# Turning the accumulated modulation of the next layer on VectorE instead of TensorE

## The chip, the core and the metric

The kernel runs on one core of a Trainium2 chip. A core has five engines that each work through their own list of instructions, strictly in order: TensorE (PE, with its weight loads shown as PEld), VectorE (DVE), ScalarE (ACT), GpSimd (POOL) and SyncE (SP), which here only issues transfers. An instruction that waits for a semaphore holds everything behind it on its engine. The metric is the device time of one execution in microseconds (us); of several runs the median counts.

## The reference, cut to what matters

The program is a two-layer trunk on 512 latent and 256 context tokens of width 1024. Each layer first derives a modulation (shift, scale and gate for two sub-layers, 6 x 1024 columns) from two vectors `c` and `c_ctx`, then does token mixing, then an MLP with 4096 hidden columns:

```python
mx = (silu_c @ w_ada[i] + b_ada[i])[:, None, :]      # latent tokens, 6*1024 columns
mc = silu_cc @ w_ada[i] + b_ada[i]                   # context tokens
...
x = x + gx1 * y_x                                    # token mixing
x = x + gx2 * sqrelu_mlp(modulate(rmsnorm(x, norm2_g[i]), sx2, ax2), w_mlp1[i], w_mlp2[i])
```

What the change touches is the product of two vectors with `w_ada[1]`, the modulation of the second layer. It is two rows of 6144 numbers, and the kernel needs them as columns: a number for each of 128 partitions, for 48 tiles of 128 columns and both kinds of token.

## The kernel before, in words

All matrices are float32 and are split into a high and a low part; a product is three matmuls (lines 107 to 109). Weights come in slabs of 256 columns (`r_w`), ScalarE makes the high part (`h_w`, line 76) and in layer 0 GpSimd the low part (`l_w`, line 77).

The MLP of layer 0 has four rounds. A round computes eight hidden tiles `f` from four slabs of `w_mlp1`, then adds eight tiles `r` from four slabs of `w_mlp2` to the residual stream `X`. I call one such slab a weight slab: TensorE does four blocks for it, two of 512 latent tokens (24 matmuls each) and two of 256 context tokens. An `f` block is emptied from PSUM by ScalarE into `fr` (three buffers, line 1211) and squared; VectorE then forms its low part `fl` (line 1214), which the `r` blocks need. An `r` block is emptied by VectorE alone, with the sum into `X` (line 1135); the latent blocks have two PSUM banks and the context blocks two more. In the names `f_0_4_0` and `r_0_2_512` the numbers are the round, the tile, and the first token of the block.

Between these blocks `ada_rows` works on the modulation of layer 1, in 24 modulation slabs of 256 columns, each loaded in two halves `ar` of 512 KB (line 245). `ar` has one buffer, so a load starts when the products of the half before it have read it. For each half and each of the two vectors, ScalarE (line 258, the first product of a slab) and VectorE (line 261) multiply by a number per partition and add up in `adaac`, a tile of 128 partitions by 512 numbers with four buffers in turn (tag `t2k`). After the two halves a slab's 1024 rows are folded into 128 partitions. What is left is a sum over partitions and a turn: TensorE transposes the four 128 x 128 pieces into a PSUM tile `adaps` (line 270), and VectorE reduces it (line 273) and adds the bias (line 275).

`ada_rows` is a generator; the MLP calls a step after a latent block, one half each. But this is only the order in which the program is written. Each engine's list is put together at build time by a scheduler that estimates times, so where a step stands on an engine's list follows from that estimate and from what it waits for, such as a free buffer.

Of the kernel before, what the change touches and what calls it, by code (L numbers as in the profile page):

```python
# [8 lines left out]
F32 = mybir.dt.float32  # L9
F32R = mybir.dt.float32r  # L10
AF = mybir.ActivationFunctionType
ALU = mybir.AluOpType
AX = mybir.AxisListType

P = 128
# [24 lines left out]
R_BADA, R_N1, R_N2, R_BG, R_BDW, R_LNG, R_LNB, R_ANG, R_C, R_CC, R_END = (  # L40
    0, 48, 56, 64, 80, 84, 88, 92, 93, 101, 109)
# [5 lines left out]
def f32(ap):  # L47
    return ap.bitcast(F32)
# [3 lines left out]
def trunk_kernel(  # L52
# [6 lines left out]
    nc = tc.nc  # L59
# [3 lines left out]
    cpool = ctx.enter_context(tc.tile_pool(name="cpool", bufs=1))  # L63
# [3 lines left out]
    spool = ctx.enter_context(tc.tile_pool(name="spool", bufs=2))  # L67
# [34 lines left out]
    def rows(src, col0, ncols):  # L102
        return src[:, col0 : col0 + ncols].rearrange("(k p) n -> p k n", p=P)
# [24 lines left out]
    nc.sync.dma_start(cst, consts[:, :C_COS])  # L128
    ident = cst[:, C_ID : C_ID + P]
    ones = cst[:, C_ONE : C_ONE + P]  # L130
    mhalf = cpool.tile([P, 8], F32, name="mhalf")
    nc.gpsimd.memset(mhalf, -0.5)

# [5 lines left out]
    state = {"behind": ()}  # L139
# [100 lines left out]
    def ada_rows(i, L):  # L240


        def load(n):
            r = state["rp"].tile([P, KT // 2, 256], F32, tag="araw", bufs=1, name=f"ar{i}_{n}")
            nc.sync.dma_start(r, rows(w_ada[i], 256 * (n // 2), 256)[:, 4 * (n % 2) : 4 * (n % 2) + 4])
            return r

        r = load(0)
        for n in range(48):
            s = n // 2  # L250
            if n % 2 == 0:
                a = state["tp"].tile([P, 512], F32, tag="t2k", bufs=state["nt"], name=f"adaac{i}_{s}")
                a = a.rearrange("p (q n) -> p q n", q=2)
            for j in range(4):
                k = 4 * (n % 2) + j
                for q in range(2):
                    if k == 0:
                        nc.scalar.activation(out=a[:, q], in_=r[:, j], func=AF.Copy,
                                             scale=cvec[:, k, q : q + 1])
                    else:  # L260
                        nc.vector.scalar_tensor_tensor(  # L261
                            out=a[:, q], in0=r[:, j], scalar=cvec[:, k, q : q + 1], in1=a[:, q],
                            op0=ALU.mult, op1=ALU.add)
            if n < 47:
                r = load(n + 1)
            yield
            if n % 2:
                ps = state["mi"](f"adaps{i}_{s}")
                for m in range(4):
                    nc.tensor.transpose(ps[:, m * P : m * P + P],  # L270
                                        a[:, m // 2, m % 2 * P : m % 2 * P + P], ident)
                ad = L["ad"][:, :, 2 * s : 2 * s + 2]
                nc.vector.tensor_reduce(out=ad, in_=ps.rearrange("p (q m k) -> p q m k", q=2, m=2),
                                        axis=AX.X, op=ALU.add)
                nc.vector.tensor_tensor(
                    out=ad, in0=ad,
                    in1=L["cols"][:, R_BADA + 2 * s : R_BADA + 2 * s + 2].unsqueeze(1)
                    .to_broadcast([P, 2, 2]), op=ALU.add)

    def ada_gain(L, which, ks=slice(0, KT)):  # L280
        par, r0, nm = ((1, R_N1, "A1"), (4, R_N2, "A2"))[which]
# [71 lines left out]
    for t in range(NTT):  # L353
# [4 lines left out]
        if t == 1:  # L358
            L = layer_params(0)
# [17 lines left out]
    for t in range(NTT):  # L377
        xn = xns[t]
        nc.scalar.activation(out=xn, in_=xrs[t], func=AF.Square, accum_out=rs[:, t : t + 1])
        r = rs[:, t : t + 1]  # L380
# [9 lines left out]
    for s in range(2):  # L390
        nc.vector.tensor_tensor(
            out=cvec[:, :, s], in0=L["cols"][:, R_C + 8 * s : R_C + 8 * s + 8],
            in1=sg[:, 8 * s : 8 * s + 8], op=ALU.mult)
# [36 lines left out]
    for i in range(DEPTH):  # L430
# [5 lines left out]
        cols = L["cols"]  # L436
# [480 lines left out]
        def ps_for(g, name):  # L917
            if g.start:
                return mc.tile([P, 512], F32, tag="mc", name=name)
            return mm_tile(name)  # L920
# [52 lines left out]
        for half, lst in ((1, ga), (0, gc)):  # L973
            for s in range(4):
# [6 lines left out]
                for m in range(2):  # L981
# [3 lines left out]
                    for g in groups:  # L985
                        W = g.stop - g.start
                        ps = ps_for(g, f"gt{i}_{half}_{mb}_{g.start}")
# [70 lines left out]
        for s in range(4):  # L1058
# [3 lines left out]
            for g in groups:  # L1062
                W = g.stop - g.start
                for m in range(2):
                    mb = 2 * s + m
                    ps = ps_for(g, f"ya{i}_{mb}_{g.start}")
                    fm_block(ps[:, :W], w, m * P, lambda k: (ah[:, k], al[:, k]), g)
                    nc.vector.tensor_tensor(out=ga[mb][:, g], in0=ga[mb][:, g], in1=ps[:, :W],
                                            op=ALU.mult)
# [12 lines left out]
        for cc in range(CT):  # L1082
            for a0, W, t0 in cgr:
                low = nc.vector.tensor_tensor(out=CL[:, cc, t0 : t0 + W],
                                              in0=ca[cc][:, a0 : a0 + W],
                                              in1=f32(CH[:, cc, t0 : t0 + W]), op=ALU.subtract)
        normed.append(low.ins)
        mh, ml = [None] * KT, [None] * KT
        for s in range(2):
# [7 lines left out]
            for m in range(4):  # L1097
                mb = 4 * s + m
                for g in groups:
                    W = g.stop - g.start  # L1100
                    ps = ps_for(g, f"yc{i}_{mb}_{g.start}")
# [3 lines left out]
                                            op=ALU.mult)  # L1105
                rr = {}
                for g in groups:
                    rr[g.start] = gp.tile([P, 512], F32, tag="ar", bufs=3,
                                          name=f"mr{i}_{mb}_{g.start}")[:, : g.stop - g.start]
                    nc.vector.tensor_tensor(out=rr[g.start], in0=ga[mb][:, g], in1=gc[mb][:, g],  # L1110
                                            op=ALU.add)
# [79 lines left out]
        if not last:  # L1191
            Ln = layer_params(i + 1)
            acc = xp.tile([P, NT], F32, tag="acc", name=f"acc{i}_3")
            rpool = tc.tile_pool(name="araw", bufs=1, reuse_waits="tile")
            state["rp"] = rpool.__enter__()
            ada_todo = ada_rows(i + 1, Ln)
            hh = hpool.tile([P, KT, NT], F32R, tag="hh", name=f"h1h_{i + 1}")
            hl = hpool.tile([P, KT, NT], F32R, tag="hl", name=f"h1l_{i + 1}")
# [80 lines left out]
        if not last:  # L1279
# [3 lines left out]
            L = Ln  # L1283
# [77 lines left out]
```

## Time and profile before

| what | value |
|---|---|
| median of 3 runs | 2370.24 us (2361.84 to 2371.28) |
| profiled execution, its own time | 2368.32 us |
| profiled execution, span from first to last instruction | 2366.5 us |
| TensorE / VectorE / ScalarE / GpSimd busy | 2286.9 / 1477.9 / 992.1 / 689.4 us |
| granted TensorE clock | 0.989 |
| line 270, transposes of `adaac` | 96 matmuls, 852 to 1317 us |
| line 261, VectorE products into `adaac` | 336, 183.0 us busy |

The MLP of layer 0 with the modulation work lies between about 760 and 1370 us of the span. Idle time of an engine costs something only where another one waits for it; so the views that name who ended a wait, and the chain of waits, matter more here than the busy shares.

### The profile page before, as it was taken

How to read it: one execution, taken by the hardware profiler on the slowest of the kernel's cores; microseconds unless marked ns; L12 is line 12 of the kernel's file. 1: busy time of each engine (PE TensorE's matmuls, PEld its weight loads, DVE VectorE, ACT ScalarE, POOL GpSimd, SP SyncE). 2: the span in 40 equal slices, each digit the busy share in tenths (PEclk: the TensorE clock that was granted, in tenths of full speed). 3: DMA queues.
4: the chain of work that ended last, by engine and by line, in shares of the span. 5: the costliest groups of instructions: out<-in, count | busy, mean ns of one | idle time of the engine just before them, and what ended most of it. 6: DMA issues, size and time to landing. Idle time of an engine off the chain costs nothing.

```text
span 2366.5 us, 36536 instructions
## 1 busy us (share of the span) xinstructions
PE 2286.9 (97%) x14698; PEld 2049.6 (87%) x14698; DVE 1477.9 (62%) x2581; ACT 992.1 (42%) x1965; POOL 689.4 (29%) x792
## 2 busy tenths in 40 slices
PE   7999999999999999999999998999999999999999
PEld 6999998888888988888888997999877879888887
DVE  6777776699666665555563366676759976433333
ACT  5555654522332353242514345555542333532432
POOL 2866754100000133232232365766610000000000
PEclk9999999999999999999999999999999999999999
DMA  9211111144535223334332211111123324232322
GB/s 306 60 43 35 44 45 44 46 159 135 173 114 186 84 81 124 117 115 133 108 112 85 90 55 56 43 43 41 43 76 126 129 88 127 82 97 92 104 89 71
DMA packets 222570, 224.76 MB, mean 95 GB/s; under 512 B 6256, under 2 KB 212544, under 8 KB 222272
## 3 DMA queue, kind: packets, MB, share of 16 engines
q1 hardware_dynamic: 222400, 222.43, 29.2%
q8 instruction: 115, 1.88, 0.3%
q14 instruction: 55, 0.45, 0.1%
HBM read 208.73 MB, written 13.67 MB: 94 GB/s over the span
## 4 chain that ended last, share of the span: by engine, by line
PE 81%; DVE 10%; DMA 3%; ACT 3%; POOL 2%; issue 1%; SPq 0%; ACTq 0%; DVEq 0%; POOLq 0%
PE r L107 6%; PE r L108 6%; PE r L109 6%; PE f L108 6%; PE f L107 6%; PE f L109 5%; PE gt L107 3%; PE gt L109 3%; PE gt L108 3%; PE qk L107 2%; PE qk L108 2%; PE qk L109 2%; PE v L107 2%; DVE adaac L261 2%; PE v L108 2%; PE v L109 2%
## 5 line engine op out<-in xcount | busy, mean ns | idle before, releaser
L108 PE MATMUL f<-h2l,h_w 128*128 128x512 f32 (+1 forms) x832 | 284.0, 343 | 3.8 <-DVE h2l L326 2.0
L107 PE MATMUL r<-fh,h_w 128*128 128x512 f32 (+1 forms) x832 | 283.9, 342 | 0.4 <-DVE X L1135 0.4
L107 PE MATMUL f<-h2h,h_w 128*128 128x512 f32 (+1 forms) x832 | 282.3, 343 | 2.0 <-ACT h2h L76 1.3
L108 PE MATMUL r<-fl,h_w 128*128 128x512 f32 (+1 forms) x832 | 283.2, 340 | 0.1
L109 PE MATMUL r<-fh,l_w 128*128 128x512 f32 (+1 forms) x832 | 282.9, 340 | 0.0
L109 PE MATMUL f<-h2h,l_w 128*128 128x512 f32 (+1 forms) x832 | 282.5, 341 | 0.0
L77 POOL TENSOR_TENSOR l_w<-r_w,h_w 128x1024 fp32r<-128x1024 f32 x64 | 158.1, 2492 | 348.4 <-ACT h_w L76 348.4
L261 DVE SCALAR_TENSOR_TENSOR adaac<-ar,cvec,adaac 128x256 f32<-128x256 f32 x336 | 183.0, 597 | 89.3 <-DMA ar<-in_w_ada_dram 64.2
L76 ACT ACTIVATE h_w<-r_w 128x1024 fp32r<-128x1024 f32 x128 | 128.5, 1051 | 261.5 <-PE r L108 117.2
L940 DVE SCALAR_TENSOR_TENSOR cacc<-z,cols,cacc 128x783 f32<-128x783 f32 (+1 forms) x240 | 201.1, 890 | 0.3
L107 PE MATMUL qk<-h_wqk,h1h 128*128 128x256 f32 x640 | 183.9, 289 | 5.1 <-ACT h1h L76 3.6
L108 PE MATMUL qk<-l_wqk,h1h 128*128 128x256 f32 x640 | 181.3, 285 | 0.0
L108 PEld LDWEIGHTS f<-h2l,h_w 128*128 128x128 f32 x832 | 158.3, 190 | 22.9 <-POOL h2l L77 3.0
L109 PE MATMUL qk<-h_wqk,h1l 128*128 128x256 f32 x640 | 177.1, 285 | 0.0
L107 PEld LDWEIGHTS f<-h2h,h_w 128*128 128x128 f32 x832 | 156.7, 190 | 20.6 <-ACT h2h L76 1.9
L109 PEld LDWEIGHTS f<-h2h,l_w 128*128 128x128 f32 x832 | 158.1, 190 | 17.7
L108 PEld LDWEIGHTS r<-fl,h_w 128*128 128x128 f32 x832 | 157.8, 190 | 17.5 <-DVE fl L1214 0.5
L109 PEld LDWEIGHTS r<-fh,l_w 128*128 128x128 f32 x832 | 157.6, 190 | 17.7
L107 PEld LDWEIGHTS r<-fh,h_w 128*128 128x128 f32 x832 | 157.6, 190 | 17.7 <-issue 0.5
L707 DVE TENSOR_REDUCE st<-S 128x1 f32<-128x768 f32 (+1 forms) x160 | 134.7, 846 | 61.1 <-PE S L705 60.0
L1135 DVE SCALAR_TENSOR_TENSOR X<-r,ad,X 128x512 f32<-128x512 f32 (+1 forms) x104 | 64.8, 625 | 172.8 <-PE r L109 172.5
L710 ACT ACTIVATE e<-S,st 128x768 f32<-128x768 f32 (+1 forms) x160 | 130.8, 820 | 36.3 <-DVE st L707 36.2
(253 smaller groups left out, 6245.2 us busy)
## 6 DMA issues: line engine op xcount, KB each, us to landing
r_w<-in_w_mlp_dram SPq DMA_DIRECT2D x64, 1024.0 KB, 5.5
ada<-in_w_ada_dram SPq DMA_DIRECT2D x24, 1024.0 KB, 5.8
ar<-in_w_ada_dram SPq DMA_DIRECT2D x48, 512.0 KB, 3.7
r_wqk<-in_w_in_dram SPq DMA_DIRECT2D x32, 512.0 KB, 5.2
r_wg<-in_w_in_dram SPq DMA_DIRECT2D x16, 1024.0 KB, 5.2
r_wv<-in_w_in_dram SPq DMA_DIRECT2D x8, 1024.0 KB, 5.2
r_wao<-in_w_attn_out_dram SPq DMA_DIRECT2D x8, 1024.0 KB, 5.2
r_wo<-in_w_out_dram SPq DMA_DIRECT2D x8, 1024.0 KB, 7.6
```

Source lines behind the costliest of these rows:

```text
L76: nc.scalar.activation(out=hi, in_=src, func=AF.Copy)
L77: (lo_eng or nc.vector).tensor_tensor(out=lo, in0=src, in1=f32(hi), op=ALU.subtract)
L107: nc.tensor.matmul(ps, sh, mh, start=first, stop=False)
L108: nc.tensor.matmul(ps, sh, ml, start=False, stop=False)
L109: nc.tensor.matmul(ps, sl, mh, start=False, stop=last)
L261: nc.vector.scalar_tensor_tensor(out=a[:, q], in0=r[:, j], scalar=cvec[:, k, q : q + 1], in1=a[:, q], op0=ALU.mult, op1=ALU.add)
L707: nc.vector.tensor_reduce(out=st[:, m : m + 1], in_=S[:, :nkey], axis=AX.X, op=ALU.max, negate=True)
L710: nc.scalar.activation(out=e[:, :nkey], in_=S[:, :nkey], func=AF.Exp, bias=st[:, m : m + 1], accum_out=st[:, 2 + m : 3 + m])
L940: nc.vector.scalar_tensor_tensor(out=ca[cc][:, :CV], in0=zt[cc][:, t : t + CV], scalar=wcol, in1=ca[cc][:, :CV], op0=ALU.mult, op1=ALU.add)
L1135: nc.vector.scalar_tensor_tensor(out=X[:, mb, g], in0=ps[:, :W], scalar=gate[:, s, mb : mb + 1], in1=X[:, mb, g], op0=ALU.mult, op1=ALU.add)
```

## The change

The transposes on TensorE go. When a slab's sum is complete, VectorE turns it in blocks of 32 by 32 into `adat` (the same `t2k` buffers) and reduces over the 32 numbers of each block into `part` (`adp` in the trace; one buffer, a tag shared with the norms' `dg`). That leaves four groups of 32 partitions to be added, which is done for eight slabs at once: four small products with `fold32`, a matrix of 128 x 32 that is made once at the start, write one PSUM tile, and one VectorE operation adds the bias for all eight slabs. So there are three folds, after modulation slabs 7, 15 and 23.

```diff
+    fold32 = cpool.tile([P, 32], F32, name="fold32")
+    nc.vector.tensor_reduce(out=fold32, in_=ident.rearrange("p (b r) -> p r b", b=4), axis=AX.X,
+                            op=ALU.add)
...
+        def fold(s0):
+            ps = state["mi"](f"adaps{i}_{s0}")
+            for c_ in range(4):
+                nc.tensor.matmul(ps[32 * c_ : 32 * c_ + 32, :32], fold32, part[:, c_],
+                                 start=True, stop=True, tile_position=(0, 32 * c_))
+            nc.vector.tensor_tensor(
+                out=L["ad"][:, :, 2 * s0 : 2 * s0 + 16].rearrange("p q (n m) -> p n q m", n=8),
+                in0=ps[:, :32].rearrange("p (n q m) -> p n q m", n=8, q=2),
+                in1=L["cols"][:, R_BADA + 2 * s0 : R_BADA + 2 * s0 + 16]
+                .rearrange("p (n m) -> p n m", n=8).unsqueeze(2).to_broadcast([P, 8, 2, 2]),
+                op=ALU.add)
...
             if n % 2:
-                ps = state["mi"](f"adaps{i}_{s}")
-                for m in range(4):
-                    nc.tensor.transpose(ps[:, m * P : m * P + P],
-                                        a[:, m // 2, m % 2 * P : m % 2 * P + P], ident)
-                ad = L["ad"][:, :, 2 * s : 2 * s + 2]
-                nc.vector.tensor_reduce(out=ad, in_=ps.rearrange("p (q m k) -> p q m k", q=2, m=2),
-                                        axis=AX.X, op=ALU.add)
-                nc.vector.tensor_tensor(
-                    out=ad, in0=ad,
-                    in1=L["cols"][:, R_BADA + 2 * s : R_BADA + 2 * s + 2].unsqueeze(1)
-                    .to_broadcast([P, 2, 2]), op=ALU.add)
+                if s % 8 == 0:
+                    part = spool.tile([P, 4, P], F32, tag="dg", bufs=1, name=f"adp{i}_{s}")[:, :, :32]
+                b = state["tp"].tile([P, 512], F32, tag="t2k", bufs=state["nt"], name=f"adat{i}_{s}")
+                nc.vector.transpose(out=b, in_=a.rearrange("p q n -> p (q n)"))
+                nc.vector.tensor_reduce(
+                    out=part[:, :, 4 * (s % 8) : 4 * (s % 8) + 4].rearrange("p c n -> p n c"),
+                    in_=b.rearrange("p (n c r) -> p n c r", n=4, c=4), axis=AX.X, op=ALU.add)
+                if s % 8 == 7:
+                    fold(s - 7)
```

Since the scheduler lays the lists anew, the change also moves instructions. On VectorE, in the first round's `r` blocks, this stood in the list before (`adaac_6` and `adaac_7` are modulation slabs 6 and 7, `ar_13` and `ar_14` halves of their weights):

```order
L261 SCALAR_TENSOR_TENSOR adaac_6_10713<-ar_13_10722,cvec,adaac_6_10713 128x256 x8
L1135 SCALAR_TENSOR_TENSOR X_8446<-r_0_2_0_10200,ad_139,X_8446 128x512
L1135 SCALAR_TENSOR_TENSOR X_8446<-r_0_3_0_10236,ad_139,X_8446 128x512
L1135 SCALAR_TENSOR_TENSOR X_8446<-r_0_2_512_10280,ad_139,X_8446 128x256
L1135 SCALAR_TENSOR_TENSOR X_8446<-r_0_3_512_10306,ad_139,X_8446 128x256
L1135 SCALAR_TENSOR_TENSOR X_8446<-r_0_4_0_10340,ad_139,X_8446 128x512
L1135 SCALAR_TENSOR_TENSOR X_8446<-r_0_5_0_10376,ad_139,X_8446 128x512
L273 TENSOR_REDUCE ad_9370<-adaps_3_10402 128x2x2
L261 SCALAR_TENSOR_TENSOR adaac_7_10869<-ar_14_10830,cvec,adaac_7_10869 128x256 x2
```

And this stands there with the change (line 277 is what was line 261, line 1149 what was 1135):

```order
L1149 SCALAR_TENSOR_TENSOR X_8448<-r_0_2_0_10195,ad_141,X_8448 128x512
L288 TENSOR_REDUCE adp_0_9946<-adat_6_10841 128x4x4
L277 SCALAR_TENSOR_TENSOR adaac_7_10844<-ar_14_10809,cvec,adaac_7_10844 128x256 x6
L1149 SCALAR_TENSOR_TENSOR X_8448<-r_0_3_0_10231,ad_141,X_8448 128x512
L1149 SCALAR_TENSOR_TENSOR X_8448<-r_0_2_512_10271,ad_141,X_8448 128x256
L277 SCALAR_TENSOR_TENSOR adaac_7_10844<-ar_15_10853,cvec,adaac_7_10844 128x256 x7
L1149 SCALAR_TENSOR_TENSOR X_8448<-r_0_3_512_10297,ad_141,X_8448 128x256
L277 SCALAR_TENSOR_TENSOR adaac_7_10844<-ar_15_10853,cvec,adaac_7_10844 128x256
L287 STREAM_TRANSPOSE adat_7_10993<-adaac_7_10844 128x512
L288 TENSOR_REDUCE adp_0_9946<-adat_7_10993 128x4x4
L277 SCALAR_TENSOR_TENSOR adaac_8_11002<-ar_16_10961,cvec,adaac_8_11002 128x256 x2
L1149 SCALAR_TENSOR_TENSOR X_8448<-r_0_4_0_10331,ad_141,X_8448 128x512
```

Slab 7 stood behind the sum into `X` of `r_0_5_0`; now all of it, and two products of slab 8, stand ahead of the sum of `r_0_4_0`. It goes on like this: slabs 7, 8 and 9 are ahead of the sum of `r_0_7_0`, slabs 10 and 11 ahead of the low part of `f_1_2_0`; slabs 12 to 18 stand between the low parts of `f_1_5_0` and `f_2_0_0`; slabs 20 to 22 and most of 23 between the low part of `f_2_6_0` and the sum of `r_2_4_0`.

On TensorE, a group of transposes stood after each weight slab or so. The one for slab 7 stood behind the last matmul of `f_1_5_0`:

```order
L109 MATMUL f_1_5_0_10988<-h2h_8456,l_w_0_1_2_10943 128x512
L270 MATMUL adaps_7_11018<-cst,adaac_7_10869 128x128 x4
L107 MATMUL f_1_4_512_11036<-h2h_8456,h_w_0_1_2_10942 128x256
L108 MATMUL f_1_4_512_11036<-h2l_8457,h_w_0_1_2_10942 128x256
L109 MATMUL f_1_4_512_11036<-h2h_8456,l_w_0_1_2_10943 128x256
```

Now the first fold stands at that same place, and nothing stands where the other seven groups were:

```order
L109 MATMUL f_1_5_0_10963<-h2h_8458,l_w_0_1_2_10918 128x512
L250 MATMUL adaps_0_10996<-adp_0_9946,fold_77 32x32 x4
L107 MATMUL f_1_4_512_11013<-h2h_8458,h_w_0_1_2_10917 128x256
L108 MATMUL f_1_4_512_11013<-h2l_8459,h_w_0_1_2_10917 128x256
L109 MATMUL f_1_4_512_11013<-h2h_8458,l_w_0_1_2_10918 128x256
```

Elsewhere little moves. In layer 1, which has no modulation work, some convolution taps and weight splits change places on VectorE, and the three products of the convolution's LayerNorm (lines 1012, 1030 and 300) stand up to two blocks later on TensorE.

## Prediction

> **What bounds the kernel now.** First the page: the busy shares, and the shares of the chain that ended last.
>
> ```profile
> PE 2286.9 (97%) x14698; PEld 2049.6 (87%) x14698; DVE 1477.9 (62%) x2581; ACT 992.1 (42%) x1965; POOL 689.4 (29%) x792
> PE 81%; DVE 10%; DMA 3%; ACT 3%; POOL 2%; issue 1%; SPq 0%; ACTq 0%; DVEq 0%; POOLq 0%
> ```
>
> TensorE is the bound over the span, yet a tenth of the chain is VectorE's. To see whether the change touches that tenth I read the chain in order of time (start us, us, what), in the first round of layer 0's MLP, and an earlier piece of it from a wider window.
>
> ```profile
> 874.53 0.52 ACT adaac L258
> ...
> 890.71 3.56 DMA ar<-in_w_ada_dram
> 894.29 0.52 ACT adaac L258
> ...
> 909.31 0.52 ACT adaac L258
> ...
> 925.73 0.52 ACT adaac L258
> 926.27 1.68 DVE adaac L261 x4
> 927.95 0.40 DVE X L1135
> 928.35 4.69 DVE adaac L261 x2
> 933.09 3.54 DMA ar<-in_w_ada_dram
> 936.72 3.25 DVE adaac L261 x8
> 939.98 0.67 DVE X L1135
> 940.78 0.47 PE r L107
> ```
>
> This chain is not TensorE's. It is the modulation loop: a load, ScalarE's first product, VectorE's products, and only then the next load, because `ar` has one buffer. It ends at 940.78 in a matmul that waited for the sum into `X`, which stood on VectorE's list behind slab 6. TensorE's timeline prices that wait, and the waits of 862 to 1317 us (who waited for whom: us in total, times, longest) say what holds the loop afterwards.
>
> ```profile
> 940.78 0.47 PE L107 MATMUL r<-fh,h_w 128*128 128x512 f32 x1 [0.35 <-DVE X L1135]
> ACT adaac L258 <- PE adaps L270: 33.0, 6, 10.0
> DVE ad L273 <- PE adaps L270: 23.7, 9, 5.4
> PE adaps L270 <- DVE adaac L261: 2.0, 2, 1.1
> ```
>
> So VectorE's list had used up its whole lead at 940 us, and cost 0.35. Then it recovers, since the loop is held back: ScalarE waits 33.0 us to begin a slab because `adaac`'s buffers are freed by TensorE's transposes. Those transposes are what keeps the loop in step with TensorE, and they are what the change removes. The step is read from the chain:
>
> ```profile
> 1100.04 0.44 PE adaps L270 x4
> 1117.20 0.44 PE adaps L270 x4
> 1134.33 0.44 PE adaps L270 x4
> ```
>
> A group each 17.13 us, 0.44 of it the transposes, leaves 16.69 for a weight slab: about 5.46 for each latent block and 2.88 for each context block (24 matmuls at 0.2275 and 0.12; 2 x 8.34). The loop's own pace, free of TensorE, is read from ScalarE's starts above: slab 3 took 19.8 us (874.53 to 894.29), slab 4 15.0, slab 5 16.4. Slab 6 would have come to 18.0: 14.2 to its last product, 3.7 for the next load and 0.1 around it.
>
> **The change part by part.** Durations first (line, engine, operation, tiles: min/median/max in ns), a load's flight, and three timeline or chain rows.
>
> ```profile
> L261 DVE SCALAR_TENSOR_TENSOR adaac<-ar,cvec,adaac x336: 468/478/2626, 768.1 to 1257.1; 128x256 f32<-128x256 f32 x168
> L273 DVE TENSOR_REDUCE ad<-adaps x24: 676/682/693, 853.2 to 1317.1; 128x4 f32<-128x512 f32 x24
> L275 DVE TENSOR_TENSOR ad<-ad,cols x24: 148/158/2391, 856.4 to 1317.8; 128x4 f32<-128x4 f32 x24
> L542 DVE TENSOR_REDUCE rqk<-sqe x80: 404/417/427, 60.8 to 1708.2; 128x4 f32<-128x260 f32 x80
> L383 DVE TENSOR_SCALAR xn<-xr,rs x6: 735/748/754, 7.7 to 30.9; 128x1024 f32<-128x1024 f32 x6
> DMA to landing us min/median/max: 3.4/3.7/8.3
> 927.67 5.08 POOL L77 TENSOR_TENSOR l_w<-r_w,h_w 128x1024 fp32r<-128x1024 f32 x2 [9.78 <-ACT h_w L76]
> L1135 DVE SCALAR_TENSOR_TENSOR X<-r,ad,X x104: 471/737/753, 920.8 to 2360.6; 128x512 f32<-128x512 f32 x56, 128x256 f32<-128x256 f32 x48
> 852.84 0.41 DVE L162 COPY cols<-smps 128x256 f32<-128x256 f32 x1
> 735.37 1.93 PE L219 MATMUL adaps<-ada,cvec 128*32 128x256 f32 x30
> 807.84 0.34 PE nc_n L311 x4
> ```
>
> *Removed from TensorE*: 24 groups at 0.44, 10.6 us. Not all of it lies on the path. Groups 0 to 2 stand where TensorE waits for VectorE anyway:
>
> ```profile
> 855.96 0.39 PE L108 MATMUL f<-h2l,h_w 128*128 128x256 f32 x1 [1.76 <-DVE h2l L326]
> 868.44 0.44 PE L270 MATMUL adaps<-cst,adaac 128*128 128x128 f32 x2 [0.88 <-DVE adaac L261]
> 870.94 0.44 PE L270 MATMUL adaps<-cst,adaac 128*128 128x128 f32 x2 [1.14 <-DVE adaac L261]
> ```
>
> The two waits of group 2 (2.0 us) go too, but the loop paces this stretch up to 940 us, so a TensorE that is earlier waits later, at the `r` blocks. I count these three groups and the 2.0 us as nothing; they are worth 3.3 us if VectorE has room. Removed: 21 x 0.44 = 9.2.
>
> *Added to TensorE*: three folds of four small products, each two instructions as the products of line 219 are. An instruction costs 0.064 (1.93 over 30) to 0.085 (0.34 over 4), so a fold costs 0.5 to 0.7; I take the upper, 2.0 for three.
>
> *On VectorE* a slab loses the reduction (0.68) and the bias (0.16), and gains a block transpose and a reduction from SBUF. The reduction: 0.42 for 260 numbers and 0.68 for 512, so 0.68. The transpose stands in no trace here; a copy of 256 numbers takes 0.41, an operation on 1024 takes 0.75, and I take 0.68, near the upper. That is 24 x 0.52 = 12.5 us more, but it comes behind the slab's last product, while the next load flies for 3.7 us: 1.36 fits in there. I count 0. Without that cover it is 12.5.
>
> *ScalarE's* work stays. The fold matrix is one reduction at the very start, where TensorE waits 5.7 us for the first input anyway:
>
> ```profile
> PE xT L367 <- DMA xr<-in_x_dram: 5.7, 1, 5.7
> ```
>
> *The brake goes.* This decides. Nothing of TensorE stands between slabs 0 and 7 any more; slab 8 can begin as well, and only the reductions into `part` wait for a fold. The loop's instructions now stand as much earlier on VectorE's list as the scheduler thought them able to run, with the sums into `X` and the low parts behind them. Where the loop is slower than that, TensorE waits for banks.
>
> Stretch A, from the sum of `r_0_2_0` to that of `r_0_7_0`: three slabs (7, 8, 9). TensorE needs the rest of a slab, one slab and two blocks, 11.2 + 16.7 + 10.9 = 38.8 us. A latent bank must be free again 11.2 us after its block (one latent and two context blocks later), but that lead is gone at the start, as the 0.35 showed. Slabs 5 and 6, just ahead and of the same kind, mean 17.2: 3 x 17.2 - 38.8 = 12.8. Slabs 10 and 11 want 34.4 against 27.9 up to `f_1_2_0`; ScalarE empties `f` banks and there are three `fr` buffers, so of those 6.5 I count 2. A: 15.
>
> Stretch B, between the low parts of `f_1_5_0` and `f_2_0_0`: seven slabs, against 5.8 + 5 x 16.7 + 5.5 = 94.7 us, and about 13 that the `fr` buffers give. At 15.7 (slabs 4 and 5): 109.9 - 107.7 = 2.
>
> Stretch C, from `f_2_6_0` to the sum of `r_2_4_0`: 3.75 slabs, and first the bias and four late operations behind the second fold (2.9), against 50.1 + 11.2 of lead. It lies in `r` blocks as slab 6 did: 3.75 x 18.0 + 2.9 - 61.3 = 9.
>
> What makes the loop slow beside its load is GpSimd: its two `l_w` operations take 5.08, and the two products of VectorE in that time took 4.69 instead of 0.8. The sums into `X` read one operand from PSUM and were never held: at most 0.753.
>
> *Layer 1* has its taps in another order. TensorE idles 2.6 us in that hundred, so I allow 2.6 either way and count 0:
>
> ```profile
> 1860.00:1960.00 100.00, 97.38 (x441) 78.66 (x440) 76.92 (x111) 37.34 (x50) 1.93 (x1) 1.00 0.31 103
> ```
>
> **Sum.** -9.2 + 2.0 + 15 + 2 + 9 = +18.8. Against the profiled execution's 2368.3 that is 2387; the median of the runs lies 1.9 above it, so I say 2388.
>
> **The rivals.**
>
> *VectorE keeps up* (not slower): bare, a slab is two loads of 3.7, one product of ScalarE (0.52) and 14 of VectorE at 0.40 (3.25 over 8), 13.5. Then A is 1.7, B and C nothing, and group 2's waits stay gone: -9.2 - 2.0 + 2.0 + 1.7 = -7.5, 2361. It decides from 13.6 us a slab downwards. Against it: all four slabs that ran free took 15.0 or more. For it: with the brake on, VectorE is busy only 98.4 of 202 us later on (stretch, then TensorE, weight loads, VectorE and so on):
>
> ```profile
> 1115.00:1317.00 202.00, 202.00 (x1187) 179.14 (x1186) 98.41 (x183) 76.25 (x132) 57.31 (x24) 1.00 0.32 102
> ```
>
> *Only the first stretch, and mildly*: at 15.0, the shortest seen, A is 6.2, B and C 0: -1.0, 2367.
>
> *The loop loses everywhere*: at slab 6's 18.0, A is 17, B 18 (7 x 18.0 - 107.7), C 9: 44 - 7.2 = +37, 2405. It would be so if a transpose or reduction also had to wait for GpSimd. The reduction of line 542 reads one SBUF operand and never took over 427 ns, so I doubt it for the reduction; for the transpose no row speaks.
>
> On this the Trainium skill (SBUF — State Buffer, the section on who interferes with whom) states that a VectorE instruction with at most one SBUF input, outside the two-port modes, does not contend with GpSimd, and it does not list a transpose among the operations with such modes. By that rule the transpose runs beside GpSimd, and the 0.18 below for this rival would fall to some 0.1; the trace agrees for the reduction and cannot say for the transpose.
>
> **How the numbers follow.** Forecast (2380 to 2397) 0.52; everywhere 0.18; mild 0.18; keeps up 0.12. The range for 8 in 10 takes in the mild case and most of the high one: 2366 to 2411. A measurement here tells some 0.5%, 11.9 us, from no change, so slower means above 2382: 0.52 x 0.93 + 0.18 = 0.66, and a little of the mild case, 0.67. Faster means below 2358.4: half of keeping up, 0.07. The rest is 0.26.
>
> **What would show it.** Right: matmuls of `r` that wait for `X`, several us each, in the first and third round, and `f` or `r` waiting for `fl`; on VectorE, waits for `ar` just ahead of those sums; no `adaps` among ScalarE's waits; the next layer starting later. Wrong: TensorE without gaps in 940 to 1230 us, each weight slab 16.7, the span shorter by 7; or a transpose far above 0.75. If the loss stands in layer 1, the moved taps did it and not the loop.

## The result and the profile after

The changed kernel takes 2385.7 us (median of six runs, 2385.1 to 2386.9) against 2365.9 us of the kernel before in the same comparison. The ratio is 1.0078, with a 95% interval of 1.0065 to 1.0091: slower by 19.8 us. The prediction was 2388 us, slower, with a range of 2366 to 2411.

The page of the changed kernel: busy shares, then the shares of the chain that ended last, by engine and by line.

```profile
PE 2283.2 (96%) x14626; PEld 2043.4 (86%) x14626; DVE 1501.9 (63%) x2585; ACT 991.4 (42%) x1965; POOL 690.6 (29%) x792
PE 70%; DVE 14%; DMA 8%; ACT 4%; POOL 3%; issue 1%; SPq 0%; ACTq 0%; DVEq 0%; POOLq 0%
DVE adaac L277 7%; DMA ar<-in_w_ada_dram 6%; PE f L107 4%; PE f L108 4%; PE f L109 4%; PE r L107 4%; PE r L108 4%; PE r L109 4%; PE gt L107 3%; PE gt L109 3%; PE gt L108 3%; PE qk L107 2%; PE qk L108 2%; PE qk L109 2%; PE v L107 2%; PE o L109 2%
```

TensorE does less work than before (2283.2 us for 2286.9), and yet the span is 17.4 us longer. Its share of the chain fell from 81% to 70%. What took the place stands first in the list by line: VectorE's products into `adaac` and the loads into `ar`, the modulation loop. VectorE itself is busy for 24.0 us more (1501.9 for 1477.9), still at 63%; what counts is where its work stands.

What TensorE waited for in layer 0's MLP, 750 to 1400 us (us in total, times, longest):

```profile
PE r L107 <- DVE X L1149: 13.8, 4, 7.8
PE f L107 <- DVE X L1149: 2.6, 2, 1.3
PE f L107 <- ACT fr L1225: 2.1, 4, 1.1
```

In the kernel before, the same view had 0.4 us for `r` and nothing for `f` behind `X`. The four waits of `r` are two pairs, one in the first round of the MLP and one in the third. The longest stands in this piece of the chain (start us, us, what):

```profile
1231.56 4.23 DVE adaac L277 x5
1235.79 0.40 DVE X L1149
1236.18 2.16 DVE adaac L277
1238.39 3.86 DMA ar<-in_w_ada_dram
1242.34 4.10 DVE adaac L277 x4
1246.44 0.67 DVE X L1149
1247.25 0.77 PE r L107
1248.02 0.43 PE r L108
...
1251.43 0.43 PE r L107
1251.86 0.28 PE r L108
1252.36 0.23 PE r L107
```

A sum into `X` stands on VectorE's list behind four products of the next half slab, these wait for a load of 3.86 us, and TensorE waits for the bank that the sum frees: the chain of the prediction, with 7.8 us instead of 0.35 at its end. One thing in it was not predicted: the products behind the wait come every 0.43 us instead of 0.23, up to 1251.86.

The work that moved, by line (engine, operation, tiles: min/median/max in ns, first and last start):

```profile
L287 DVE STREAM_TRANSPOSE adat<-adaac x24: 697/711/715, 782.9 to 1248.7; 128x512 f32<-128x512 f32 x24
L288 DVE TENSOR_REDUCE adp<-adat x24: 674/680/690, 854.3 to 1249.5; 128x16 f32<-128x512 f32 x24
L277 DVE SCALAR_TENSOR_TENSOR adaac<-ar,cvec,adaac x336: 446/478/2647, 769.4 to 1248.2; 128x256 f32<-128x256 f32 x168
```

The turn and the reduction cost 0.71 and 0.68 and vary by 18 ns at most, while the products beside them are held up to 2.65 us.

Comparing the start of the same blocks of TensorE in the two traces gives the loss by place (changed less before, us; a block's products are found in a trace by their order in the program):

| block (first product) | before, us | later by |
|---|---|---|
| `f_0_3`, context | 871.1 | -0.5 |
| `r_0_1`, latent | 912.4 | -1.0 |
| `r_0_5`, latent | 946.3 | +3.6 |
| `f_1_1`, latent | 980.5 | +7.0 |
| `r_1_7`, latent | 1100.2 | +5.4 |
| `f_2_2`, context | 1140.1 | +7.6 |
| `r_2_2`, context | 1208.5 | +6.5 |
| `r_2_6`, latent | 1231.4 | +15.8 |
| `r_2_7`, latent | 1236.9 | +18.0 |
| `f_3_4`, context | 1294.0 | +16.4 |
| `v_2_4` of layer 1 | 1595.6 | +14.9 |
| end of the span | 2366.5 | +17.4 |

### The profile page after: what moved, and what is told of

It reads as the page before. It is cut to its first block, busy times and chain, and to the rows that moved or that the text cites. A ratio compares the mean times of both kernels' runs of the same rounds, so it can differ in the third digit from the quotient of the medians.

```text
span 2383.9 us, 36385 instructions
## 1 busy us (share of the span) xinstructions
PE 2283.2 (96%) x14626; PEld 2043.4 (86%) x14626; DVE 1501.9 (63%) x2585; ACT 991.4 (42%) x1965; POOL 690.6 (29%) x792
## 4 chain that ended last, share of the span: by engine, by line
PE 70%; DVE 14%; DMA 8%; ACT 4%; POOL 3%; issue 1%; SPq 0%; ACTq 0%; DVEq 0%; POOLq 0%
DVE adaac L277 7%; DMA ar<-in_w_ada_dram 6%; PE f L107 4%; PE f L108 4%; PE f L109 4%; PE r L107 4%; PE r L108 4%; PE r L109 4%; PE gt L107 3%; PE gt L109 3%; PE gt L108 3%; PE qk L107 2%; PE qk L108 2%; PE qk L109 2%; PE v L107 2%; PE o L109 2%
## 5 line engine op out<-in xcount | busy, mean ns | idle before, releaser
L107 PE MATMUL r<-fh,h_w 128*128 128x512 f32 (+1 forms) x832 | 285.5, 344 | 14.0 <-DVE X L1149 13.8
L277 DVE SCALAR_TENSOR_TENSOR adaac<-ar,cvec,adaac 128x256 f32<-128x256 f32 x336 | 191.5, 627 | 121.0 <-DMA ar<-in_w_ada_dram 71.4
L108 PEld LDWEIGHTS r<-fl,h_w 128*128 128x128 f32 x832 | 159.0, 191 | 17.7
L1228 DVE TENSOR_TENSOR fl<-fr,fh 128x512 fp32r<-128x512 f32 (+1 forms) x104 | 69.1, 669 | 130.2 <-ACT fr L1227 130.2
```

The costliest lines, as they stand in the source:

```text
L107: nc.tensor.matmul(ps, sh, mh, start=first, stop=False)
L108: nc.tensor.matmul(ps, sh, ml, start=False, stop=False)
L277: nc.vector.scalar_tensor_tensor(out=a[:, q], in0=r[:, j], scalar=cvec[:, k, q : q + 1], in1=a[:, q], op0=ALU.mult, op1=ALU.add)
L1228: nc.vector.tensor_tensor(out=fl[mb][:, g], in0=r[:, :W], in1=f32(fh[mb][:, g]), op=ALU.subtract)
```

## The experiments

Three theories stood at the start. Theory 1 is the prediction's: the transposes held the modulation loop in step with TensorE, and without them VectorE's list has the loop too early. Theory 2: VectorE's added turn itself costs the time. Theory 3: the folds and the single buffer `part` do. Experiments 1 to 4 shared one set of runs of the kernel before (2366.7 us), 5 to 8 another (2367.1), 9 to 12 a third (2368.8). In the comparison of the result it stood at 2365.9, so a difference in us between kernels of different sets is good to some 3 us; where it is small, the ratios and their intervals decide.

### 1. No turn at all

From the kernel before:

```diff
-                ps = state["mi"](f"adaps{i}_{s}")
-                for m in range(4):
-                    nc.tensor.transpose(ps[:, m * P : m * P + P],
-                                        a[:, m // 2, m % 2 * P : m % 2 * P + P], ident)
...
-                nc.vector.tensor_reduce(out=ad, in_=ps.rearrange("p (q m k) -> p q m k", q=2, m=2),
+                nc.vector.tensor_reduce(out=ad, in_=a.rearrange("p q (m k) -> p q m k", m=2),
```

> The kernel before without its 96 transposes; the reduction reads the sum `adaac` where it stands. Left out: the turn and the sum over partitions of the modulation, so VectorE has no work more than before, and TensorE no fold. Theory 1 (the transposes were a brake: without them the modulation loop stands too early on VectorE's list, and TensorE waits for banks behind it): no faster than the changed kernel, 2385 or more, up to 2430, since not even every eighth slab waits for TensorE; `r` blocks wait 4 to 8 us for sums into X. Theory 2 (VectorE's added turn, 24 x 0.71 us, is what costs) and theory 3 (the folds and the single buffer `part` are): before less 24 x 0.44 of transposes, 2355, and below before in any case.

Measured: 2422.0 us, ratio 1.0222 (1.0198 to 1.0246). Work was only taken away, 10.6 us of it from TensorE, and the kernel became 55 us slower. TensorE's waits in 860 to 1400 us:

```profile
PE r L107 <- DVE X L1131: 13.5, 5, 4.4
PE r L108 <- DVE fl L1210: 10.4, 3, 6.5
PE f L107 <- ACT fr L1207: 7.6, 5, 3.2
PE f L107 <- DVE X L1131: 4.3, 3, 2.5
```

This is the strongest evidence of the study. No turn on VectorE, no fold, no `part`: theories 2 and 3 both say 2355. That the loop had to wait for the transposes was worth 55 us, and up to 10.6 more that they cost. Not all of it stands where the change loses. The context part of `f_0_0` is already 15.9 us late here, at 853.7 us of the kernel before, since slab 2 begins at 804.9, while in the changed kernel it begins at 853.6 and that block is 1.6 late; the other 39 us arise in the MLP's rounds behind it.

### 2. VectorE's turn beside the transposes

From the kernel before:

```diff
+                b = state["tp"].tile([P, 512], F32, tag="t2k", bufs=state["nt"], name=f"adat{i}_{s}")
+                nc.vector.transpose(out=b, in_=a.rearrange("p q n -> p (q n)"))
                 ad = L["ad"][:, :, 2 * s : 2 * s + 2]
```

> The kernel before with VectorE's turn added beside the transposes, its output unread: 24 STREAM_TRANSPOSE, 17 us of VectorE's time, as in the change; TensorE's transposes and the order they impose stay. Theory 1: 2364 to 2371, within 5 us of before. Theory 2: the loss of the change with nothing saved, 2380 to 2396. Theory 3: as before.

Measured: 2368.8 us, ratio 1.0004 (0.9992 to 1.0017).

```profile
L273 DVE STREAM_TRANSPOSE adat<-adaac x24: 699/702/714, 780.8 to 1259.2; 128x512 f32<-128x512 f32 x24
```

The whole added work of VectorE, 24 x 0.70 = 16.8 us, is there and costs nothing that can be measured, and neither does the place that `adat` takes in the four `t2k` buffers. Theory 2 falls. That the prediction counted the turn as covered is right.

### 3. A fold after every slab

From the changed kernel (shapes cut to one slab):

```diff
-                if s % 8 == 7:
-                    fold(s - 7)
+                if s % 1 == 0:
+                    fold(s - 0)
```

> The changed kernel with a fold after every slab: VectorE's turn stays, and TensorE stands between any two slabs again, as the transposes did, with 4 products for 4 transposes (a fold is 0.5 to 0.7 us of TensorE, a group of transposes 0.44). Theory 1: near before, 2362 to 2374, 12 to 24 us below the changed kernel. Theory 2: 21 folds more than the changed kernel, 2390 to 2400. Theory 3: more folds cost more, 2395 and up.

Measured: 2378.9 us, ratio 1.0037 (1.0023 to 1.0051). That is 7 us below the changed kernel's 2385.7 although 21 folds were added, so theory 3's sign is wrong; but it is 5 us above what theory 1 allowed. TensorE's waits in 860 to 1400 us (but for 0.2 us) show that the loop is not the reason:

```profile
PE f L108 <- DVE ag L208: 2.3, 1, 2.3
PE nb_n L314 <- DVE dg_n L310: 1.9, 1, 1.9
PE f L107 <- DVE X L1149: 1.8, 1, 1.8
```

No `r` waits for `X` any more. Against before, the blocks' starts are 2.7 us late ahead of the first `r` block and 2.5 us in the last round's, so the loop's stretch costs nothing net. The loss arises ahead of it (2.8 us by layer 0's `yc` blocks) and in layer 1 (8.6 us by its `yc` blocks). What makes these two parts no run here shows, and they stay open.

### 4. The loop held on VectorE's list

From the changed kernel. The block `issue_after` only sets the order on VectorE's list; it adds no semaphore:

```diff
-            nc.vector.scalar_tensor_tensor(
+            state["vx"] = nc.vector.scalar_tensor_tensor(
                 out=X[:, mb, g], in0=ps[:, :W], ...
...
-                next(ada_todo, None)
+                with tc.issue_after(state["vx"].ins):
+                    next(ada_todo, None)
...
-                nc.vector.tensor_tensor(out=fl[mb][:, g], ...
+                state["vx"] = nc.vector.tensor_tensor(out=fl[mb][:, g], ...
```

> The changed kernel with one thing more: each piece of the modulation loop stands on VectorE's list behind the last sum into X (or low part) of the block after which the program calls it. No semaphore, no instruction more. Theory 1: the waits behind sums into X go, the removed transposes are gained: 2350 to 2362, below before. Theory 2: VectorE has the same work, so 2380 to 2390. Theory 3: 2380 to 2390 or above, since the reductions come later and the folds wait for them.

Measured: 2359.1 us, ratio 0.9952 (0.9932 to 0.9972), 27 us below the changed kernel with the same instructions, and below before. Left of the waits in 860 to 1400 us, besides 0.2 us for `fr`:

```profile
PE adaps L250 <- DVE adp L288: 2.2, 1, 2.2
PE nb_n L314 <- DVE dg_n L310: 1.9, 1, 1.9
```

Every wait for a sum into `X` is gone, with the same instructions and only VectorE's list held, so no other part of the change is needed to explain the loss. The scheduler lays the other engines' lists anew around the held one; what their moves are worth was not separated.

### 5. Held, with the folds one call later

From the kernel of experiment 4:

```diff
-                if s % 8 == 7:
-                    fold(s - 7)
+                if s == 23:
+                    fold(16)
+            elif s and s % 8 == 0:
+                fold(s - 8)
```

> The held kernel (the changed kernel with the modulation loop kept behind the sums on VectorE's list) with the first two folds issued two calls later, after the next slab has begun. In the held kernel the one wait of TensorE for the loop is 2.2 us ahead of a fold. Theory 1: that wait goes, 2353 to 2360, 0 to 4 us below the held kernel. Theory 3 (folds cost by their place): 4 us and more below it.

The edit moves a fold by one call of the generator, not by the two of the expectation: the fold of slab 7 stood behind the `yield` of the half 15 and now stands behind that of the half 16.

Measured: 2353.5 us, ratio 0.9939 (0.9925 to 0.9952). The wait ahead of the fold is gone, and between 900 and 1250 us TensorE has no gap (the stretch, then its length, then TensorE, weight loads, VectorE, ScalarE, GpSimd, granted clock, DMA share, GB/s); the same stretch of the changed kernel stands below.

```profile
900.00:1250.00 350.00, 350.00 (x2028) 309.52 (x2028) 205.54 (x403) 113.06 (x190) 102.16 (x42) 1.00 0.39 122
```

```profile
900.00:1250.00 350.00, 331.58 (x1897) 290.25 (x1896) 228.08 (x396) 106.67 (x183) 101.48 (x41) 0.98 0.37 121
```

Against experiment 4 it gains 5.5 us by the medians, where theory 1 allowed 0 to 4 for a wait of 2.2; the intervals of the two ratios overlap at their ends. From `f_2_2` to `r_2_2`, where that wait stood, the two traces differ by 3.5 us (experiment 4 falls back by 2.2 against before, experiment 5 gains 1.3): the 2.2, and 3.4 us at half clock that follow in experiment 4. No more than that is claimed.

### 6. The kernel before, held

The edit of experiment 4 on the kernel before.

> The kernel before, transposes on TensorE, with the same hold on VectorE's list. Theory 1: the transposes hold the loop already, so little moves: 2360 to 2370, and the held changed kernel stays 3 to 10 us below it (24 x 0.44 of transposes less the folds 2.0). If the hold alone made the gain of the held kernel: 2359 or less, and the change is worth nothing.

Measured: 2372.0 us, ratio 1.0021 (1.0009 to 1.0032): the hold alone gains nothing, it costs 5 us, 2 more than theory 1 allowed. In 1000 to 1320 us TensorE waits:

```profile
PE adaps L270 <- DVE adaac L261: 7.3, 3, 3.3
```

A transpose needs its slab finished when TensorE comes to it. A loop that is held back is late for that. The held changed kernel (experiment 4) is 13.0 us below this one, where the expectation had 3 to 10, and with late folds 18.5 us below. The change is worth that much under the same hold, and these waits are 7.3 of it. Whether transposes that are issued a call later as well would lose their waits too was not run.

### 7. No fold

From the changed kernel, `fold` without its products, so that the sum over the four groups of partitions is missing:

```diff
-            ps = state["mi"](f"adaps{i}_{s0}")
-            for c_ in range(4):
-                nc.tensor.matmul(ps[32 * c_ : 32 * c_ + 32, :32], fold32, part[:, c_],
-                                 start=True, stop=True, tile_position=(0, 32 * c_))
...
-                in0=ps[:, :32].rearrange("p (n q m) -> p n q m", n=8, q=2),
+                in0=part[:, 0].rearrange("p (n q m) -> p n q m", n=8, q=2),
```

> The changed kernel with the folds left out: VectorE adds the bias to `part` itself, so that the sum over the four groups of partitions is missing. TensorE has neither transposes nor folds. Theory 1: the last brakes, two folds between slabs, are gone too: not faster than the changed kernel, 2384 to 2400. Theory 3: the loss goes with the folds, 2356 to 2370.

Measured: 2397.1 us, ratio 1.0119 (1.0104 to 1.0134), 11 us above the changed kernel. Taking the folds away costs time, as theory 1 says and theory 3 excludes: by this the two folds inside the loop were its last brakes.

### 8. A fold after every second slab

> The changed kernel with a fold after every second slab, twelve in all. Theory 1 with the fold as the only price: 9 folds of 0.6 more than the changed kernel, 12 fewer than with a fold each, and a brake that is looser: TensorE may wait once or twice where the loop first runs free; 2368 to 2380. Theory 2: 2390 to 2393. Theory 3: between the changed kernel and the fold after each by the number of folds, if folds cost then above the changed kernel.

Measured: 2374.5 us, ratio 1.0022 (1.0012 to 1.0033), the edit of experiment 3 with two slabs for one. With experiments 3 and 7 it gives the dose: 24, 12, 3 and 0 folds take 2379, 2374, 2386 and 2397 us, the first two not apart by their intervals. The looser brake shows at one place only, the first round, in 860 to 1400 us:

```profile
PE r L107 <- DVE X L1149: 6.0, 3, 4.9
```

### 9. Held in the first chunk alone

From the kernel of experiment 4:

```diff
-                with tc.issue_after(state["vx"].ins):
+                with tc.issue_after(state["vx"].ins) if cch == 0 else ExitStack():
```

> The changed kernel, held as before but in the first chunk of the MLP alone (stretch A up to the sums of r_0; from f_1 on the scheduler is free again). Theory 1, if the loss belongs to the place A: A's waits go, C's stay, 2370 to 2378. If the loss belongs to the freedom, wherever it begins: the loop first runs free one chunk later and the waits of A stand at the r_1 blocks, 2380 to 2395, no gain on the changed kernel.

Measured: 2396.7 us, ratio 1.0113 (1.0096 to 1.0130), 1.7 us over the upper end of the second expectation and above the changed kernel. The stretch A is clean: TensorE waits 0.2 us in 860 to 1010 us. Then, one chunk later:

```profile
1046.29 0.79 PE L108 MATMUL r<-fl,h_w 128*128 128x512 f32 x1 [4.74 <-DVE fl L1229]
1051.88 0.79 PE L108 MATMUL r<-fl,h_w 128*128 128x512 f32 x1 [3.95 <-DVE fl L1229]
```

The loss does not belong to A. It starts wherever the loop is set free, and the loop, held till then, has more slabs left on which to lose; that this makes it worse than the changed kernel is argued, not shown.

### 10. Held from the third chunk on

The same edit with `cch >= 2`.

> The changed kernel, held from the third chunk on (f_2, r_2, f_3, r_3), free in A and B. Theory 1: A's waits stand as in the changed kernel (4 to 8 us by r_0_7), the 7.8 us wait of r_2_6 and the slow products behind it go: 9 to 13 us below the changed kernel, 2372 to 2377. If the third chunk's loss is only what A left behind: 2384 to 2388.

Measured: 2376.4 us, ratio 1.0031 (1.0021 to 1.0042), 9.3 us below the changed kernel. In 860 to 1112 us the waits of A stand:

```profile
PE r L107 <- DVE X L1149: 6.0, 3, 4.7
```

In 1112 to 1400 us TensorE waits for the loop only at a fold:

```profile
PE adaps L250 <- DVE adp L288: 2.2, 1, 2.2
```

So what lies behind the second chunk, C above all, is worth 9.3 us net of that 2.2. A is not smaller for it: in this trace, the slowest of the ten runs, the starts from `r_0_1` to `f_1_1` fall back by 10.4 us, in the changed kernel's by 8.0.

### 11. Two load buffers

From the changed kernel: pieces of two `k` rows for four, two buffers of half the size.

```diff
-            r = state["rp"].tile([P, KT // 2, 256], F32, tag="araw", bufs=1, name=f"ar{i}_{n}")
+            r = state["rp"].tile([P, KT // 4, 256], F32, tag="araw", bufs=2, name=f"ar{i}_{n}")
...
-            if n < 47:
-                r = load(n + 1)
+                if j % 2 and n < 47:
+                    r2[j // 2] = load(2 * n + 2 + j // 2)
```

> The changed kernel with each half of a modulation slab loaded in two pieces of 256 KB into two buffers (the same memory), so that the next piece flies while VectorE multiplies the other; 96 loads for 48. A slab of the free loop then takes some 7 us less of flight, 12 to 14 for 18. Theory 1 with the pace as the cause: 2368 to 2380, 6 to 18 below the changed kernel. If it is the order alone and the scheduler sets the quicker loop so much earlier: 2384 and above. Theory 2: no change, 2384 to 2388, VectorE's work is the same.

Measured: 2391.3 us, ratio 1.0089 (1.0071 to 1.0107): no gain. The 5.5 us above the changed kernel are no difference by the ratios (1.0078, 1.0065 to 1.0091). The loop did become quick: from slab 5 on ScalarE begins a slab every 10.0 to 14.1 us, for 13.8 to 20.7 in the changed kernel, leaving out the gaps in which the loop stands (60 and 70 us here, 32 there). It did not help, since the scheduler sets the quicker loop so much earlier. TensorE's waits in 860 to 1400 us:

```profile
PE r L107 <- DVE X L1150: 17.6, 9, 4.9
PE r L108 <- DVE fl L1229: 3.4, 2, 2.5
```

My expectation from the pace fell here, and it sharpened theory 1. How many slabs' products stand ahead of a sum into `X` on VectorE's list can be counted in the order of the programs. From the sum of `r_0_0` to that of `r_0_7` (latent parts) TensorE needs three weight slabs and a block, 3 x 16.69 + 5.46 = 55.5 us by the prediction's rows. What the list asks of the loop in that time, and what the loop does by ScalarE's starts:

| kernel | slabs ahead of `r_0_0` | of `r_0_7` | asked, us a slab | the loop in that stretch, us a slab |
|---|---|---|---|---|
| before | 5.9 | 8.0 | 26 | held by the transposes |
| changed | 5.9 | 10.0 | 13.5 | 16.1 to 18.4 |
| no turn (1) | 9.4 | 13.4 | 13.9 | 15.1 to 19.2 |
| two buffers (11) | 7.0 | 12.0 | 11.1 | 11.7 to 14.0 |
| held (4) | 1.4 | 5.0 | 15.4 | 16.0 to 20.3 (5) |

The last row takes the loop's pace from experiment 5, which holds it in the same way; there nothing waits, because the products stand behind the sums. In the changed kernel the list asks for 13.5 us a slab, just what the prediction worked out for a bare slab without GpSimd's hold, and no slab of that kernel is that quick.

### 12. Held, late folds, two buffers

The edits of experiments 5 and 11 together.

> The held kernel with late folds and with the two small load buffers. Theory 1: with the hold no wait of TensorE for the loop is left but the last fold, so a quicker loop brings 0 to 4 us: 2349 to 2354. If the loop's pace still cost there: 2349 or less. If 48 more loads on SP's queue hold up the weights: 2356 and above.

Measured: 2353.9 us, ratio 0.9925 (0.9908 to 0.9943). Against experiment 5 (0.9939, 0.9925 to 0.9952) that is no difference that these runs can tell. With the order right, no cost of the loop's pace can be seen any more. Either version beats both kernels. The simpler one, experiment 5, lies 11 to 18 us below before by its interval (2367.1 x 0.0048 and x 0.0075), and 32 us below the changed kernel by the medians (2385.7 - 2353.5).

## Why the prediction was right, step by step

**The removed transposes, -9.2.** Right in price: where nothing else happens the changed kernel gains 0.44 a slab, as from the context part of `r_1_0` (+6.7) to the latent part of `r_1_7` (+5.4), three groups. The first three groups counted as nothing were nothing (-0.5 at `f_0_3`). In the held kernel they do pay: experiment 5 goes from 0.8 us ahead of before at the context part of `f_0_0` to 6.6 at `f_0_3`. The prediction gave 3.3 of those 5.8 if VectorE had room; the rest was not taken apart.

**The folds, +2.0.** Too dear. The chain of the changed kernel has a fold in its place, four products with their eight records:

```profile
1027.31 0.23 PE f L109
1027.54 0.20 PE adaps L250 x8
1027.73 0.32 PE f L107
```

With some 0.1 more on each neighbour, by the starts in the timeline, that is 0.4 a fold, 1.2 for three, for the 0.5 to 0.7 taken from the nearest rows.

**VectorE's turn, 0.** Right, by experiment 2. The estimated 0.68 for the transpose was 0.71. The rival in which the transpose also waits for GpSimd had no row for or against it. Now all 24 took 697 to 715 ns, but they say little, since only one of them overlaps one of GpSimd's `l_w` operations, here wholly inside it:

```profile
870.73 0.71 DVE L287 STREAM_TRANSPOSE adat<-adaac 128x512 f32<-128x512 f32 x1
867.72 5.25 POOL L77 TENSOR_TENSOR l_w<-r_w,h_w 128x1024 fp32r<-128x1024 f32 x2 [2.60 <-ACT h_w L76]
```

The Trainium skill (SBUF — State Buffer, the section on who interferes with whom) says that a VectorE instruction with one SBUF input, outside the two-port modes, does not contend; the trace agrees for this one transpose, and the others do not test it.

**The brake goes, +26.** The mechanism is shown by experiments 1, 4 and 7: take the brake without the work and the time rises, hold the order and it falls. By place, with the transposes that went in each stretch added back:

| stretch | predicted | measured | from |
|---|---|---|---|
| A | 15 | 8.9 | -1.0 to +7.0, two groups of 0.44 |
| B | 2 | 3.1 | +5.4 to +7.6, two groups of 0.44 |
| C | 9 | 11.9 | +6.5 to +18.0, one group of 0.44 |

In A and C these are the waits of `r` and `f` behind `X`, and the slow products behind the two long ones:

```profile
939.83 0.47 PE L107 MATMUL r<-fh,h_w 128*128 128x512 f32 x1 [0.49 <-DVE X L1149]
949.93 0.80 PE L107 MATMUL r<-fh,h_w 128*128 128x512 f32 x1 [4.39 <-DVE X L1149]
...
1227.92 0.50 PE L107 MATMUL r<-fh,h_w 128*128 128x512 f32 x1 [1.14 <-DVE X L1149]
...
1247.25 0.77 PE L107 MATMUL r<-fh,h_w 128*128 128x512 f32 x1 [7.81 <-DVE X L1149]
```

C is 1.14 + 7.81 = 9.0 of waits, as predicted, and some 2.1 of slow products (nine at 0.43 instead of 0.23, two partly so), a term that the prediction did not have. A is the term that was mis-sized: with 1.3 at `f_1_1` its waits are 6.2, and some 2.4 of slow products come on top. The prediction took 17.2 us a slab for slabs 7 to 9, from the two just ahead. ScalarE's starts in the changed kernel lie 18.4, 16.4 and 13.8 us apart there, 48.5 for three where 51.6 was taken; by the prediction's own formula that leaves 48.5 - 38.8 = 9.7, for waits of 6.2, so TensorE seems to have had some lead left too, where the prediction took none. Of the 2 us for slabs 10 and 11 at most 0.5 appeared, TensorE's idle time in 988 to 1112 us. The errors nearly cancel, 23.9 for 26. The sum had +18.8 over before, and the runs gave +19.8. That the total came so near is in part luck: A was 6 us too dear, C and layer 1 some 3 us each too cheap, and the sum itself has a slip, since 2368.3 + 18.8 + 1.9 is 2389 and not 2388, and the rivals' times leave out the 1.9.

**Layer 1, 0 ± 2.6.** From `v_2_4` (+14.9) to the end (+17.4) it lost 2.5. That is at the edge of what was allowed. Whether the moved taps or the scatter of a run did it is open: in the held kernel of experiment 5, with the same code there, the same stretch kept its lead (17.2 us at `v_2_4`, 17.7 at the end).

**The signs and the rivals.** The waits of `r` for `X` in the first and third round, the loads ahead of those sums and the later layer 1 came as listed, and ScalarE waits for no `adaps`; but no product waited for a low part `fl`, only `f` for a bank behind `X`. "VectorE keeps up" was to decide from 13.6 us a slab downwards. Experiment 11 brought the loop to 11 to 14 and the time still did not fall, so that condition was wrong as stated: the pace must be held against what the list asks, and the list asks more of a quicker loop. "The loop loses everywhere" did not happen here, and did where more brakes were taken: 2397 without folds, 2422 without any turn; its mechanism there was not GpSimd on the transpose, which experiment 1 does not have, but the freedom itself.

## What to carry to other kernels

An instruction that costs an engine time can also be what keeps another engine's list in step; before it is removed, ask what it makes wait, and put an order in its place. Here the same change is worth -14 us with an order on VectorE's list and +20 us without it. Where an in-order engine mixes work that others wait for with filler work, count how much filler the list puts ahead of each urgent instruction, and how fast it asks the filler to run: in experiment 11 a quicker filler did not help, since the scheduler only set it earlier.

## What was not expected of the hardware

After some waits TensorE's products come at half rate. In the kernel without any turn (experiment 1) they show the start and the end of it (start us, us, instruction, the wait ahead of it):

```profile
997.74 0.50 PE L107 MATMUL r<-fh,h_w 128*128 128x512 f32 x1 [1.79 <-DVE X L1131]
...
998.77 0.59 PE L108 MATMUL r<-fl,h_w 128*128 128x512 f32 x1
999.16 0.63 PE L109 MATMUL r<-fh,l_w 128*128 128x512 f32 x1
...
1002.14 0.43 PE L107 MATMUL r<-fh,h_w 128*128 128x512 f32 x1
1002.42 0.39 PE L108 MATMUL r<-fl,h_w 128*128 128x512 f32 x1
```

From 998.77 to 1002.14 the starts lie 0.43 apart, and after that 0.23 again: 3.4 us at half rate, beginning 1 us after a wait of 1.79. With two buffers (experiment 11) a longer wait was followed by none:

```profile
1114.07 0.47 PE L107 MATMUL r<-fh,h_w 128*128 128x512 f32 x1 [3.44 <-DVE X L1150]
```

So the length of the wait alone does not decide. Where it falls does, as the granted clock shows (the stretch, its length, then TensorE busy, and after the other engines the granted clock; experiment 1 above, experiment 11 below):

```profile
995.40:998.81 3.41, 1.61 (x8) 1.02 (x7) 3.41 (x3) 0.00 (x0) 3.41 (x2) 1.00 0.00 0
998.81:1002.22 3.41, 3.41 (x10) 2.64 (x9) 1.12 (x2) 0.00 (x0) 0.44 (x1) 0.50 0.40 122
```

```profile
1108.98:1112.39 3.41, 1.66 (x14) 1.45 (x13) 1.95 (x6) 0.49 (x2) 0.00 (x0) 1.00 0.52 151
1112.39:1115.80 3.41, 1.73 (x8) 1.45 (x9) 3.12 (x8) 0.00 (x0) 0.00 (x0) 1.00 0.38 107
```

In each trace the stretches at half clock begin and end whole multiples of 3.413 us apart, so there is a grid that runs on whatever the kernel does. The wait of 1.79 lay inside one cell of it, idle for 1.80 of 3.41, and the next cell had the half clock. The wait of 3.44 fell on both sides of 1112.39, 1.75 and 1.68 idle, and neither cell was followed by half clock. Over all fourteen traces, past the first 60 us, no cell at full clock with more than 1.84 idle was followed by a full one, and none with less than 1.26 by a half one: about half a cell of idle time decides. In the changed kernel the granted clock is 0.90 in 1212 to 1262 us, around the wait of 7.8.

The Trainium skill (TensorE: Matmul & The Clock Gate, Part 1 on the clock gate) states half rate after an idle window of about 3.4 us, products of 512 columns then 426.7 ns apart, and a window that runs freely. The rate, the 3.4 us and the free running agree with these rows. The idle time does not: about half a window was enough. For a sum of waits it means a surcharge that a sum of the waits alone leaves out: 2.4 us behind the wait of 4.39 in A and 2.1 behind that of 7.81 in C.
